# Products reordered by pass in a two-layer hybrid backbone, with a sub-layer's first product begun ahead of its last head tile

## The chip, the cores and the metric

One core of one Trainium2 chip runs the whole program in one launch. The metric is the device time of that launch in microseconds. Lower is better.

## The reference, cut to what matters

Two consecutive layers of a diffusion backbone act on 256 latent tokens and 256 context tokens of width 1024, in float32. Each layer is a feed-forward half-step, a token mixer, and a second feed-forward half-step, each modulated before and normalised after:

```
h = LN(x) * (1 + scale) + shift
a, u = split(h @ w_in)              # w_in: 1024 x 5632
y = (silu(a) * u) @ w_out           # w_out: 2816 x 1024
x = LN(alpha * x + 0.5 * gate * y) * g + b
```

Layer 0 mixes with a Fourier transform over half of the channels and a long convolution over the rest. Layer 1 mixes with two bidirectional gated scans (GLA with 4 heads of 64, HGRN2 with 4 heads of 128), and only its latent tokens go on to the last feed-forward half-step. The decay gate of GLA is a product of rank 16 per direction (`af @ a_up`).

## The kernel before, in words

The 512 tokens are four tiles of 128: tiles 0 and 1 are latents, 2 and 3 the context. `hT[k]` holds the modulated input of a sub-layer, feature-major, for eight blocks k of 128 features; each block is kept as a high part and a low part, both in the one-pass format `fp32r`. A weight unit (128 x 1024, 512 KB) is loaded by SP into one of three `raw` buffers; ScalarE (ACT) casts its high part (L78), and VectorE (DVE) subtracts to get the low part (L79). A float32 product is then three products that accumulate (`mm3`, L459): high x high, high x low, low x high. `Stream` (L39) keeps the order of the units: `get` takes the next one and splits up to two ahead, `split_to` and `split_spare` split further ahead. Units marked spare are split into the large pool `S`, the others into three buffers.

Everything is issued from one program order per engine, and each engine works its own list off in order. Background generators wait in `bg`; `step(n)` issues their next pieces between products, `flush()` issues all that is left.

A sub-layer starts with a head (`tm_head`, L522). It takes token tiles in turn: for tile t it runs four weight units against `hT` of that tile (24 products of 512 columns). In the meantime the last tiles are still being closed by `close` (L438): post-norm, norm (`xn`), transposes on TensorE (PE) into `ptr` (L411), scale and shift into `hm` (L428 on DVE or L430 on ACT), the split into `hT` (L226 on ACT, L227 on DVE or POOL). `due(t)` issues the transposes and what follows of tile t. In tile 2, `due(3)` is issued after the second unit (key `d`, L544) or, if the norm has not been issued by then, with a `flush()` at the key `F` (L548), and right behind it `split_to` splits the first units that follow the head (L551). After the head come the feature-major units (`fm_unit`, L464), each 24 products of 512 columns over all four tiles.

`tok_out` (L476) is the output projection: for each weight unit k all tiles of a pair, and for the last `tail` units tile by tile. `tm_mm` (L514) serves `tm_group` (L1364), the `rc` loop (L1443) and `chunk` (L1494).

The odd mixer (L1094) runs four `fm_lat` units (256 columns) for the queries, issues `due(2)` after the first (key `od2`, L1135), two more units with `due(3)` in each, and then the decay unit `pab` (L1152), which needs all four tiles of `hT`. `attend(j, tt)` (L1319) makes the scores `pF` on PE (L1331), masks them on DVE (`am`, L1338 to L1342), and forms `po` (L1348, L1351); for j = 0 the heads have 64 rows, two heads to a block of 128.

`mixer_close` (L1576) ends a mixer with `tok_out`, all of whose units are tail. In layer 1 it is followed by `ffn_lat`, whose head has eight units and two tiles.

Of the kernel before, what the change touches and what calls it, by code (L numbers as in the profile page):

```python
# [18 lines left out]
P = 128  # L19
# [109 lines left out]
def kernel(ctx: ExitStack, tc: tile.TileContext, a, out, stop=None):  # L129
# [346 lines left out]
    def tok_out(lhs, nk, tiles, fill=None, tail=0, done=None, cuts=None, hmajor=False):  # L476


        cols = {t: [slice(0, 512), slice(512, 1024)] for t in tiles}
        if cuts:  # L480
            cols[tiles[-1]] = cuts
        y = {t: [PS("y")[:, 0:c.stop - c.start] for c in cols[t]] for t in tiles}

        def mm(t, w, k, i):
            hh, hl = lhs(k, t)
            c = cols[t][i]
            mm3(y[t][i], hh, hl, w[0][:, c], w[1][:, c], k == 0, k == nk - 1)

        for k in range(nk - tail):
            w = ws.get()  # L490
            for t in tiles:
                for i in range(len(cols[t])):
                    mm(t, w, k, i)
            if fill:
                fill(k)
        held = {}
        last = ws.pos + tail
        limit = last
        while limit < len(ws.units) and ws.units[limit][2]:
            limit += 1  # L500
        ks = range(nk - tail, nk)
        for n, t in enumerate(tiles if tail else ()):
            nc_ = range(len(cols[t]))
            for i, (h, k) in enumerate([(h, k) for h in nc_ for k in ks] if n or hmajor else [(h, k) for k in ks for h in nc_]):
                if k not in held:
                    held[k] = ws.get(limit)
                mm(t, held[k], k, h)
                if fill and i % 2 and i < 2 * len(ks):
                    fill(ks[i // 2])
            if done:  # L510
                done(t, y[t])
        return y

    def tm_mm(y, w, kp, t):  # L514

        for kk in range(2):
# [3 lines left out]
            mm3(y, x[:, 0], x[:, 1], w[0][:, c], w[1][:, c], k == 0, k == KD - 1)  # L520

    def tm_head(tiles, done, n=1):  # L522

# [5 lines left out]
        for t in tiles:  # L529
# [57 lines left out]
    def ffn(l, i, extra=(), head=None):  # L587
# [7 lines left out]

        todo = (head or tm_head)(range(NT), done)
        bg.extend(extra)
        for f in range(2, KF):
# [3 lines left out]
            if f == 5 and stop == "head":  # L602
                return hs
            pa, pu = PS("pa"), PS("pu")
            fm_unit(pa)
            if todo:
# [253 lines left out]
    def even_mixer():  # L860
# [10 lines left out]

        tm_head(range(NT), done_a)

        def conv(g):

            for i in range(4):
                if i % 2 == 0:
                    pair = S([P, 2, T], name="cv")
                pu = PS("pu")
                fm_unit(pu)  # L880
                pv = pu.rearrange("p (s t) -> p s t", s=2)
# [203 lines left out]
    def queue_odd():  # L1085
        for f in range(17):
            ws.add(a["od_fm"][f], True, f < g_("SPN", 4), g_(f"qoi{f}", int(f in (1, 3, 4) or f > 5 and f % 2 == 1)))
        for n in range(4):
# [5 lines left out]
    def odd_mixer():  # L1094
        ab_c = Q([P, 2, 2], name="abc")
        sy.dma_start(out=ab_c, in_=a["gla_a_b"])
        aup = H([32, 2, 256], name="aup")
        sy.dma_start(out=aup, in_=a["gla_up"])
# [22 lines left out]
        def fm_lat(n):  # L1121

            o = PS("ql")[:, 0:L]
            hi, lo = ws.get()
            for k in range(KD):
                x = hT[k][:, :, 0:L]
                mm3(o, hi[:, P * k:P * k + P], lo[:, P * k:P * k + P], x[:, 0], x[:, 1], k == 0, k == KD - 1)
            step(n)
# [23 lines left out]
        pab = PS("pab")  # L1152
        fm_unit(pab)
        ab = H([32, T], name="ab")
        act.copy(ab, pab[0:32, :])
        E, U = [], []
# [162 lines left out]
        def attend(j, tt):  # L1319
# [5 lines left out]
            pa = [[PS("pF") for _ in range(nh // 2)] for _ in range(2)]  # L1325
            for n, f, r, hd in lst:
                for d in range(2):
                    qk, xx = QK[d, j], XX[d, j]
                    for c in (d, 1 - d):
                        kk = (qk if c == d else xx)[r, 1, f, P * tt:P * tt + P]  # L1330
                        pe.matmul(pa[d][n // 2][:, P * (n % 2) + 64 * c:P * (n % 2) + 64 * c + 64], lhsT=kk,  # L1331
                                  rhs=qk[r, 0, f, P * tt + 64 * c:P * tt + 64 * c + 64], start=True, stop=True)
            yield
            z = az[turn[0] % 2]
# [10 lines left out]
            po = [PS("po") for _ in range(nh // 2)]  # L1345
            for n, f, r, hd in lst:
                oc = po[n // 2][:, P * (n % 2):P * (n % 2) + P]
                pe.matmul(oc, lhsT=am[:, P * n:P * n + P], rhs=v[tt][:, P * hd:P * hd + P], start=True, stop=False)  # L1348
                for d in range(2):
                    s = 0 if (d == 0) == (tt == 0) else 1  # L1350
                    pe.matmul(oc, lhsT=XX[d, j][r, 0, f, P * tt:P * tt + P], rhs=ST[d, j][r, s, f, :],  # L1351
                              start=False, stop=d == 1)
            if j == 0:
# [222 lines left out]
    def mixer_close(l, tiles, nxt):  # L1576
# [7 lines left out]

        def done(t, y):
            if t == tiles[-1]:
                ws.split_spare(ws.pos + g_(f"{k0}a", 3))
                flush()
            else:
                ws.split_spare(ws.pos + g_(f"{k0}A{t}", 0))  # L1590
                older.append(t - 1)
            if t == tiles[0]:
# [10 lines left out]
        older = []  # L1603
        tok_out(lhs, KD, tiles, fill, KD, done, None, g_(f"{k0}h", 0))
# [209 lines left out]
def lay_out(inputs):  # L1814
# [66 lines left out]
    up[0:16, 0], up[16:32, 1] = i["gla_a_up"][0]  # L1881
    o["gla_up"] = up
    o["gla_a_b"] = i["gla_a_b"][0].reshape(2, 2, P).transpose(2, 0, 1)
# [28 lines left out]
```

## Time and profile before

| | us |
|---|---|
| median of 3 runs (1817.42 to 1825.67) | 1823.25 |
| the profiled execution's own time | 1824.63 |
| its span, first to last instruction | 1822.8 |

| engine | busy us | share | instructions |
|---|---|---|---|
| PE products | 1744.2 | 96% | 8204 |
| PE weight loads (overlap the products) | 1414.9 | 78% | 8204 |
| DVE | 1256.4 | 69% | 1818 |
| ACT | 713.3 | 39% | 1048 |
| POOL | 252.9 | 14% | 273 |

Each product is one record on PE, with a weight load of its own. A float32 product that is not in the one-pass format stands as two records. A record's duration includes its way through the array, so that successive records overlap: what a product costs in a stream is the time from its start to the next one's start. The chain that ended last names only the closing instructions of the program, so the stages are read from waits, windows and timelines.

### The profile page before, as it was taken

To read this page: it belongs to the slowest core of one execution; us is meant where nothing else is said; L and a number is where in the kernel's file an instruction comes from. 1 tells how busy PE (TensorE), PEld (TensorE's weight loads), DVE (VectorE), ACT (ScalarE), POOL (GpSimd) and SP (SyncE) were. 2 spreads that over 40 slices of the span, in tenths; PEclk is the share of its full clock that TensorE was granted. 3 is DMA by queue.
4 is the path that set the end of the run, shared out by engine and by line. 5 is a ranking of instruction groups with operands and counts; after the bars stand their busy time and mean duration, and the time that the engine had idled before them with its cause. 6 is when DMAs were issued, how large, how long until landed. Compare 5 with 4: busy or idle time off the path is not lost. (4 is left out here: it accounts for less than half of the span.)

```text
span 1822.8 us, 21896 instructions
## 1 busy us (share of the span) xinstructions
PE 1744.2 (96%) x8204; PEld 1414.9 (78%) x8204; DVE 1256.4 (69%) x1818; ACT 713.3 (39%) x1048; POOL 252.9 (14%) x273
## 2 busy tenths in 40 slices
PE   6999999998999999999999999999998999989998
PEld 5788888777766788888887788888877778767887
DVE  6788887676788677777477677733576594666755
ACT  5432233453323433323335423233355463444443
POOL 1223311011000111111001111111011241110000
PEclk9999999999999999999999999999999999889999
DMA  9645756653124055554655455435554223446664
GB/s 329 226 179 199 253 218 235 219 178 139 59 88 144 24 205 211 185 189 169 219 187 173 163 212 201 173 105 196 194 177 141 81 93 92 143 139 219 208 213 134
DMA packets 91498, 314.90 MB, mean 173 GB/s; under 512 B 10848, under 2 KB 11584, under 8 KB 91392
## 3 DMA queue, kind: packets, MB, share of 16 engines
q1 hardware_dynamic: 85952, 297.09, 47.0%
q0 software_dynamic: 4576, 15.91, 2.8%
q8 instruction: 64, 1.05, 0.2%
q10 hardware_dynamic: 864, 0.51, 0.1%
q14 instruction: 42, 0.34, 0.1%
HBM read 308.18 MB, written 4.24 MB: 171 GB/s over the span
## 5 line engine op out<-in xcount | busy, mean ns | idle before, releaser
L79 DVE TENSOR_TENSOR wlo<-raw,whi 128x1024 fp32r<-128x1024 f32 x332 | 415.3, 1254 | 321.6 <-ACT whi L78 321.4
L78 ACT CAST whi<-raw 128x1024 fp32r<-128x1024 f32 x332 | 346.8, 1051 | 338.5 <-PE y L462 122.8
L243 DVE SCALAR_TENSOR_TENSOR mt<-mraw,cb 128x1024 bf16<-128x1024 f32 x256 | 309.7, 1250 | 2.5 <-DMA mraw<-in_mod_w_dram 2.5
L462 PE MATMUL pu<-hT,wlo 128*128 128x512 f32 x576 | 224.7, 390 | 3.2 <-DVE wlo L79 3.2
L460 PE MATMUL pu<-hT,whi 128*128 128x512 f32 x576 | 225.7, 392 | 0.0
L461 PE MATMUL pu<-hT,whi 128*128 128x512 f32 x576 | 224.4, 390 | 0.0
L460 PE MATMUL pa<-hT,whi 128*128 128x512 f32 x480 | 187.8, 391 | 0.0
L462 PE MATMUL pa<-hT,wlo 128*128 128x512 f32 x480 | 187.1, 390 | 0.0
L461 PE MATMUL pa<-hT,whi 128*128 128x512 f32 x480 | 187.0, 390 | 0.0
L461 PE MATMUL y<-wlo,hh 128*128 128x512 f32 x468 | 183.2, 391 | 3.8 <-DVE wlo L79 3.8
L460 PE MATMUL y<-whi,hh 128*128 128x512 f32 x468 | 183.1, 391 | 0.0
L462 PE MATMUL y<-whi,hh 128*128 128x512 f32 x468 | 182.5, 390 | 0.0
L226 ACT CAST hh<-sa 128x256 fp32r<-128x256 f32 x120 | 42.8, 404 | 296.0 <-DVE sa L614 296.0
L227 POOL TENSOR_TENSOR hh<-sa,hh 128x256 fp32r<-128x256 f32 x120 | 86.3, 739 | 516.5 <-ACT hh L226 507.1
L462 PEld LDWEIGHTS pu<-hT,wlo 128*128 128x128 f32 x576 | 108.1, 188 | 26.6 <-DVE wlo L79 4.1
L460 PEld LDWEIGHTS pu<-hT,whi 128*128 128x128 f32 x576 | 108.1, 188 | 23.5 <-ACT hh L226 0.8
L461 PEld LDWEIGHTS pu<-hT,whi 128*128 128x128 f32 x576 | 108.2, 188 | 22.8 <-issue 0.5
L461 PEld LDWEIGHTS y<-wlo,hh 128*128 128x128 f32 x468 | 87.9, 188 | 24.9 <-DVE wlo L79 7.0
L460 PEld LDWEIGHTS pa<-hT,whi 128*128 128x128 f32 x480 | 90.1, 188 | 19.7 <-issue 0.9
L234 POOL TENSOR_TENSOR rstd<-rp,mhalf 128x1 f32<-128x1 f32 x42 | 35.4, 846 | 500.8 <-DVE rp L233 494.7
L462 PEld LDWEIGHTS pa<-hT,wlo 128*128 128x128 f32 x480 | 90.1, 188 | 18.8
L461 PEld LDWEIGHTS pa<-hT,whi 128*128 128x128 f32 x480 | 90.1, 188 | 18.5
(396 smaller groups left out, 3022.3 us busy)
## 6 DMA issues: line engine op xcount, KB each, us to landing
raw<-in_ffn_out_dram SPq DMA_DIRECT2D x154, 512.0 KB, 3.6
mraw<-in_mod_w_dram SPq DMA_DIRECT2D x144, 512.0 KB, 5.1
raw<-in_ffn_in_dram SPq DMA_DIRECT2D x120, 512.0 KB, 3.8
raw<-in_ffn_tm_dram SPq DMA_DIRECT2D x44, 512.0 KB, 4.2
raw<-in_od_fm_dram SPq DMA_DIRECT2D x17, 512.0 KB, 3.9
raw<-in_od_tm_dram SPq DMA_DIRECT2D x16, 512.0 KB, 3.3
raw<-in_ffn_head_dram SPq DMA_DIRECT2D x12, 512.0 KB, 4.3
raw<-in_ev_in_dram SPq DMA_DIRECT2D x12, 512.0 KB, 3.4
```

The lines of the kernel that those rows point to most:

```text
L78: self.nc.scalar.copy(hi, w)
L79: self.nc.vector.tensor_tensor(lo, w, hi.bitcast(F32), op=ALU.subtract)
L226: act.copy(dst_hi, src)
L227: (lo_eng or dve).tensor_tensor(dst_lo, src, dst_hi.bitcast(F32), op=ALU.subtract)
L234: gp.tensor_tensor(dst, t, mhalf.to_broadcast([P, n]), op=ALU.pow)
L243: dve.scalar_tensor_tensor(H([P, D], BF16, "mt"), w, 1.0, cb[s], op0=ALU.mult, op1=ALU.mult, accum_out=acc[:, s, b:b + 1])
L460: pe.matmul(o, lhsT=wh, rhs=xh, start=start, stop=False)
L461: pe.matmul(o, lhsT=wh, rhs=xl, start=False, stop=False)
L462: pe.matmul(o, lhsT=wl, rhs=xh, start=False, stop=stop)
```

## The change

- `fm_unit`, `fm_lat`, `tm_mm`, the body and the first tail tile of `tok_out`, and `tm_head` no longer run the three products of `mm3` together. They run all products of one pass (say high x high) and then all of the next.
- `first_unit`: after tile 2 of a head, the first feature-major unit is run for the columns of tiles 0 to 2 (384), and after tile 3 for the last 128 columns. It is used in both full feed-forward heads that go through `tm_head` and in the even mixer, three places.
- In these three heads `due(3)` is issued only after tile 2's last unit.
- `due(2)` in the odd mixer moves from after the first to after the third query unit.
- The decay unit is not split; it runs from the raw float32 weights, 32 columns wide, in four column groups of the array, 16 products instead of 24. The weights behind it are repeated four times, so that the sum over the groups is formed there.
- `attend` alternates between the row halves of two heads; for j = 0 one pause is gone.
- In `mixer_close` of layer 1 the splits ahead are issued from `fill`, unit by unit.

```diff
-    def fm_unit(o, view=lambda x: x):
-        hi, lo = ws.get()
-        for k in range(KD):
-            mm3(o, hi[:, P * k:P * k + P], lo[:, P * k:P * k + P], view(hT[k][:, 0, :]), view(hT[k][:, 1, :]), k == 0, k == KD - 1)
+    def fm_unit(o, c=slice(0, T), w=None):
+        w = w or ws.get()
+        for n, (a_, b_) in enumerate(((0, 0), (0, 1), (1, 0))):
+            for k in range(KD):
+                pe.matmul(o[:, c], lhsT=w[a_][:, P * k:P * k + P], rhs=hT[k][:, b_, c], start=n + k == 0, stop=n == 2 and k == KD - 1)
+        return w
...
+        def block(todo):
+            for a_, b_ in ((0, 0), (1, 0), (0, 1)):
+                for t, w, k, i in todo:
+                    pe.matmul(y[t][i], lhsT=lhs(k, t)[a_], rhs=w[b_][:, cols[t][i]], start=k + a_ + b_ == 0, stop=k == nk - 1 and b_ == 1)
...
+    OLD, NEW = slice(0, 3 * P), slice(3 * P, T)
+    def first_unit(name):
+        part = []
+        def begin():
+            part.append(PS(name))
+            part.append(fm_unit(part[0], OLD))
+        def end():
+            fm_unit(part[0], NEW, part[1])
+            return part[0]
+        return begin, end
+    def tm_head(tiles, done, n=1, between=None):
...
-            for u in range(4 * n):
+            order = ((0, 0), (1, 0), (0, 1)) if t == tiles[0] else ((0, 0), (0, 1), (1, 0))
+            for v in range(12 * n):
+                p_, u = divmod(v, 4 * n)
                 if u not in w:
                     w[u] = ws.get(limit)
-                tm_mm(y[u // 4], w[u], u % 4, t)
+                for kk in range(2):
+                    k = 2 * (u % 4) + kk
+                    pe.matmul(y[u // 4], lhsT=hT[k][:, order[p_][0], P * t:P * t + P], rhs=w[u][order[p_][1]][:, 512 * kk:512 * kk + 512],
+                              start=p_ == 0 and k == 0, stop=p_ == 2 and k == KD - 1)
+                if v % 3 < 2:
+                    continue
+                u = v // 3
...
-                if u == g_(f"{k0}d{t}", 4 * n - 3):
+                if u == g_(f"{k0}d{t}", 4 * n - 3) and not (between and t == tiles[-2]):
                     due(t + 1)
...
-                if t == tiles[-2] and u == g_(f"{k0}F", 4 * n - 2):
+                if t == tiles[-2] and u == (4 * n - 1 if between else g_(f"{k0}F", 4 * n - 2)):
                     flush()
                     due(t + 1)
                     ws.split_to(ws.pos + g_(f"{k0}A", 1))
             if todo:
                 run(todo)
             todo = done(t, *y)
+            if between and t == tiles[-2]:
+                between()
...
-            if i == g_("od2", 0):
+            if i == g_("od2", 2):
                 due(2)
...
-        fm_unit(pab)
+        w = ws.get()
+        for n in range(2):
+            for k in range(KD):
+                j = k % 4
+                pe.matmul(pab[32 * j:32 * j + 32, :], lhsT=w[:, P * k:P * k + 32], rhs=hT[k][:, n, :].bitcast(F32),
+                          start=n == 0 and k < 4, stop=n == 1 and k >= 4, tile_position=(0, 32 * j))
...
-            yield
+            if j:
+                yield
...
+            if l and "y" not in seen:
+                ws.split_to(first + (4, 5, 7, 8, 9, 10, 11, 11)[k])
```

## Rows read from the trace of the kernel before

**Rows 1.** The page, part 1: busy us, share of the span, instructions.

```profile
PE 1744.2 (96%) x8204; PEld 1414.9 (78%) x8204; DVE 1256.4 (69%) x1818; ACT 713.3 (39%) x1048; POOL 252.9 (14%) x273
```

**Rows 2.** Waits of PE, whole run: us in total, times, longest.

```profile
PE ptr L411 <- ACT xn L398: 13.1, 10, 4.8
PE hd L460 <- ACT hT L226: 9.0, 6, 5.4
PE y L461 <- DVE lo L79: 4.8, 7, 1.1
...
PE pt L900 <- DVE cv L886: 4.4, 3, 2.2
...
PE y L461 <- DVE wlo L79: 4.2, 8, 0.8
PE pu L462 <- DVE wlo L79: 3.2, 2, 1.7
...
PE ya L461 <- DVE wlo L79: 1.7, 3, 0.8
```

**Rows 3.** Timeline of PE, from four stretches: start, us, then engine, line, tiles, count.

```profile
447.11 0.39 PE L460 MATMUL hd<-hi,hT 128*128 128x512 f32 x1
447.34 0.39 PE L461 MATMUL hd<-lo,hT 128*128 128x512 f32 x1
...
1390.07 0.28 PE L462 MATMUL ql<-hT,lo 128*128 128x256 f32 x1
1390.19 0.28 PE L460 MATMUL ql<-hT,hi 128*128 128x256 f32 x1
...
1511.04 0.39 PE L1331 MATMUL pF<-qk 128*128 128x64 f32 x2
1511.27 0.39 PE L1331 MATMUL pF<-qk,xx 128*128 128x64 f32 x2
...
21.96 1.52 PE L1661 MATMUL pm<-mraw,cst 128*32 128x128 f32 x48
```

**Rows 4.** Windows: length, then busy per engine, PEclk, DMA share, GB/s.

```profile
439.50:443.70 4.20, 4.14 (x15) 3.33 (x16) 1.37 (x4) 3.04 (x7) 0.30 (x1) 0.60 0.01 4
...
500.00:568.00 68.00, 60.41 (x226) 42.02 (x225) 60.42 (x76) 19.45 (x28) 2.18 (x4) 0.95 0.29 93
1376.00:1381.00 5.00, 0.16 (x3) 0.04 (x1) 4.27 (x9) 0.90 (x2) 0.55 (x1) 0.80 0.38 118
1381.00:1385.50 4.50, 4.50 (x21) 4.50 (x22) 3.00 (x5) 4.44 (x12) 0.00 (x0) 0.50 0.81 318
1563.00:1580.00 17.00, 17.00 (x68) 14.36 (x68) 8.57 (x15) 3.37 (x5) 2.63 (x4) 0.51 0.39 132
```

**Rows 5.** Timelines of PE and ACT at tile 3 of the three heads.

```profile
439.51 1.77 PE L411 MATMUL ptr<-ident,xn 128*128 128x128 f32 x8 [2.52 <-ACT xn L398]
...
443.73 2.96 ACT L78 CAST whi<-raw 128x1024 fp32r<-128x1024 f32 x3
...
641.04 1.04 PE L411 MATMUL ptr<-ident,xn 128*128 128x128 f32 x8
...
645.14 2.00 ACT L78 CAST whi<-raw 128x1024 fp32r<-128x1024 f32 x2
...
1016.75 1.37 PE L411 MATMUL ptr<-ident,xn 128*128 128x128 f32 x8 [0.44 <-ACT xn L398]
...
1020.57 2.01 ACT L78 CAST whi<-raw 128x1024 fp32r<-128x1024 f32 x2
```

**Rows 6.** Timelines of ACT and PE, odd mixer up to the decay unit.

```profile
1393.61 1.52 ACT L398 ACTIVATE xn<-x,nb,rstd 128x512 f32<-128x512 f32 x2 [1.04 <-DVE nb L388]
...
1406.54 0.39 PE L462 MATMUL pab<-hT,wlo 128*128 128x512 f32 x1
```

**Rows 7.** Timelines of PE and ACT, last attention and last head.

```profile
1562.83 0.46 PE L1348 MATMUL po<-vg,am 128*128 128x128 f32 x2 [2.10 <-DVE am L1342]
...
1610.82 2.92 ACT L78 CAST hi<-raw 128x1024 fp32r<-128x1024 f32 x3
```

More of the change, by code (lines that the diff above doesn't have):

```diff
@@ L503, in tok_out @@
             nc_ = range(len(cols[t]))
+            if not n and not hmajor:
+                for i, k in enumerate(ks):
+                    held[k] = ws.get(limit)
+                    block([(t, held[k], k, h) for h in nc_])
+                    if fill:
+                        fill(k)
+                if done:
+                    done(t, y[t])
+                continue
             for i, (h, k) in enumerate([(h, k) for h in nc_ for k in ks] if n or hmajor else [(h, k) for k in ks for h in nc_]):
@@ L519, in tm_mm @@
             x = hT[k][:, :, P * t:P * t + P]
-            mm3(y, x[:, 0], x[:, 1], w[0][:, c], w[1][:, c], k == 0, k == KD - 1)
-    def tm_head(tiles, done, n=1):
+            for n in range(2):
+                pe.matmul(y, lhsT=x[:, n], rhs=w[0][:, c], start=n + k == 0, stop=False)
+        for kk in range(2):
+            k = 2 * kp + kk
+            pe.matmul(y, lhsT=hT[k][:, 0, P * t:P * t + P], rhs=w[1][:, 512 * kk:512 * kk + 512], start=False, stop=k == KD - 1)
+    OLD, NEW = slice(0, 3 * P), slice(3 * P, T)
[9 more added lines that the diff above has]
+    def tm_head(tiles, done, n=1, between=None):
         w = {}
@@ L594, in done @@
             return to_features(slice(P * (t % 2), P * (t % 2) + P), [hs[t // 2][0]], h)
-        todo = (head or tm_head)(range(NT), done)
+        if head:
+            todo = head(range(NT), done)
+        else:
+            begin, end = first_unit("pa")
+            todo = tm_head(range(NT), done, 1, begin)
         bg.extend(extra)
@@ L603, in ffn @@
                 return hs
-            pa, pu = PS("pa"), PS("pu")
-            fm_unit(pa)
+            if f == 2 and not head:
+                pa = end()
+            else:
+                pa = PS("pa")
+                fm_unit(pa)
+            pu = PS("pu")
             if todo:
@@ L870, in done_a @@
             split(at[t][:, 0], at[t][:, 1], y)
-        tm_head(range(NT), done_a)
+        begin, end = first_unit("pu")
+        tm_head(range(NT), done_a, 1, begin)
         def conv(g):
@@ L878, in conv @@
                     pair = S([P, 2, T], name="cv")
-                pu = PS("pu")
-                fm_unit(pu)
+                if g + i == 0:
+                    pu = end()
+                else:
+                    pu = PS("pu")
+                    fm_unit(pu)
                 pv = pu.rearrange("p (s t) -> p s t", s=2)
@@ L1123, in fm_lat @@
             o = PS("ql")[:, 0:L]
[L1124 to L1127, printed above, removed]
+            w = ws.get()
+            for m, (a_, b_) in enumerate(((0, 0), (1, 0), (0, 1))):
+                for k in range(KD):
+                    pe.matmul(o, lhsT=w[a_][:, P * k:P * k + P], rhs=hT[k][:, b_, 0:L], start=m + k == 0, stop=m == 2 and k == KD - 1)
             step(n)
@@ L1152, in odd_mixer @@
         pab = PS("pab")
-        fm_unit(pab)
-        ab = H([32, T], name="ab")
-        act.copy(ab, pab[0:32, :])
+        w = ws.get()
+        for n in range(2):
+            for k in range(KD):
+                j = k % 4
+                pe.matmul(pab[32 * j:32 * j + 32, :], lhsT=w[:, P * k:P * k + 32], rhs=hT[k][:, n, :].bitcast(F32),
+                          start=n == 0 and k < 4, stop=n == 1 and k >= 4, tile_position=(0, 32 * j))
+        ab = H([P, T], name="ab")
+        act.copy(ab, pab)
         E, U = [], []
@@ L1325, in attend @@
             pa = [[PS("pF") for _ in range(nh // 2)] for _ in range(2)]
[L1326 to L1332, printed above, removed]
-            yield
+            for d, c, (n, f, r, hd) in [(d, c, p) for f in range(2) for d in range(2) for c in (d, 1 - d) for p in lst if p[1] == f]:
+                qk, xx = QK[d, j], XX[d, j]
+                kk = (qk if c == d else xx)[r, 1, f, P * tt:P * tt + P]
+                pe.matmul(pa[d][n // 2][:, P * (n % 2) + 64 * c:P * (n % 2) + 64 * c + 64], lhsT=kk,
+                          rhs=qk[r, 0, f, P * tt + 64 * c:P * tt + 64 * c + 64], start=True, stop=True)
+            if j:
+                yield
             z = az[turn[0] % 2]
@@ L1585, in done @@
         def done(t, y):
+            seen["y"] = t
             if t == tiles[-1]:
-                ws.split_spare(ws.pos + g_(f"{k0}a", 3))
+                if not l:
+                    ws.split_spare(ws.pos + g_(f"{k0}a", 3))
                 flush()
-            else:
+            elif not l:
                 ws.split_spare(ws.pos + g_(f"{k0}A{t}", 0))
+            if t != tiles[-1]:
                 older.append(t - 1)
@@ L1881, in lay_out @@
     up[0:16, 0], up[16:32, 1] = i["gla_a_up"][0]
-    o["gla_up"] = up
+    o["gla_up"] = np.tile(up, (4, 1, 1))
     o["gla_a_b"] = i["gla_a_b"][0].reshape(2, 2, P).transpose(2, 0, 1)
```

25 lines of the change are left out of this document (14 added, 11 removed).

## The prediction

> **What bounds the kernel now.** I read the page first: PE works on products for 96% of the span [rows 1], so there are 78.6 us in which it does not, and a change can win from these, from products that get cheaper, and from the granted clock. Then the waits of PE, which say whose lateness makes up those microseconds [rows 2]: norms of the tiles that are closed last (`ptr`), `hT` of the tile that a head takes next (`hd`), and low parts of weights (`lo`, `wlo`). Then windows, for what an idle PE loses besides [rows 4]: after the 2.5 us wait before 439.5 the granted clock is 0.60 for 4.2 us, after the wait of 1376 to 1381 it is 0.50 for 4.5 us. These are stretches at 1.2 GHz rather than 2.4; the first one lost 4.2 x (1 - 0.60) = 1.7 us of work. Last the timelines, for the order behind each wait.
>
> **What a product costs.** In a stream one starts every 0.23 us at 512 columns and every 0.12 at 256 (447.11 to 447.34, 1390.07 to 1390.19) [rows 3]. On a straight line that is 0.175 at 384 and 0.065 at 128. But products of only 64 columns start every 0.11 (two records in 0.23) [rows 3], so there is a floor which is not one of columns; for 128 I take 0.11, with 0.065 and 0.23 (no cheaper than 512) as ends. Reordering by pass leaves the number of products as it is, and each has its own weight load before and after: zero, within 0.01 us a product either way for the stationary operand that no longer repeats.
>
> The Trainium skill ("TensorE: Matmul & The Clock Gate", section "Back-to-back issue gap") gives 81 ns for a sustained stream at 128 columns; by that figure, an estimate, the sum would be 2 us lower. For 512 columns it gives 131 ns where the rows here have 230, so the rows decide.
>
> **Low parts needed later.** In the body of `tok_out` a unit's low part is now needed after 8 products, not 1, 1.6 us later; in `chunk` and in the first tail tile after 4. No single wait there is over 1.1 us. `y<-wlo` is 4.2 us in 8 waits [rows 2], of which I count five, 2.6 us, as body and gone; `ya<-wlo` 1.7, gone. `y<-lo` 4.8 us is in the tails, where each next unit arrives by DMA slower than PE asks; there the later need is earned once per tail, 3 x 0.23 = 0.7, and in two of three tails the head behind it waits for a norm whose DVE chain starts from those splits, so it is lost again: 0.7 in all. `pu<-wlo` 3.2 us is in the even mixer, where DVE is busy 60.4 of 68 us and the convolution's transposes wait for it anyway (`pt<-cv`, 4.4) [rows 2, 4]: zero. Sum: **-5.0** (0 to -9, with all of `y<-lo` and `pu`).
>
> **The three heads.** This is where I expect the loss. `flush`, `due(3)` and `split_to` stand in this order in the program before and after. So ACT casts the first unit's high part only behind tile 3's `hT`: at 443.73, 645.14 and 1020.57, done 1.0 us later, while the transposes end at 441.28, 642.08 and 1018.12 [rows 5]. Before, half of tile 2 or a quarter of it lay behind those transposes and filled that time; now all of tile 2 lies ahead, and what lies behind is the early product, which needs just that cast. PE idles 3.4 + 4.1 + 3.4 = 10.9 us, and tile 3's `hT` is ready before the early product starts, so the product covers nothing. Idle of that length has cost 1.7 us of clock [rows 4]: 3 x 1.7 = 5.1. The split itself: 24 x (0.175 + 0.11 - 0.23) = 1.4, three times 4.2 (0.3 to 12.6 by the ends above). What goes: the 2.5 us wait before 439.51 with its 1.7 of clock, 0.4 before 1016.75 [rows 5], and about 1.0 of what `hd<-hT` has besides its longest [rows 2]; 5.6. Sum 10.9 + 5.1 + 4.2 - 5.6 = **+14.6**. Queued behind the new wait is all of PE's list, tile 3's head first; ACT and DVE wait for PE only afterwards. No DMA moves in SP's or POOL's queue: the units' loads are issued by buffers that come free.
>
> **Odd mixer.** `due(2)` two units later: these are 2 x 24 x 0.12 = 5.8 us of PE work in front of a norm that is 4.8 us late [rows 2], so that wait and its 2.2 us of clock go [rows 4]. ACT's and DVE's pieces of tile 2 then stand behind tile 3's, whose norm comes some 2 us sooner than 1393.61 [rows 6]; but PE is at tile 3's transposes by about 1389, since the last query unit before them is ready then. A new wait of 3.5 us with 1.1 of clock takes its place. The decay unit: 24 x 0.23 = 5.5 before; after, `pm` has the same form at 128 columns, 48 records, 24 products, in 1.52 us, six rounds of four at 0.25 [rows 3], so four rounds at 512 columns are 4 x 4 x 0.25 = 4.0. Its raw buffer stays taken until it has run, under a window with DMA to spare. Sum -4.8 - 2.2 - 1.5 + 4.6 = **-3.9** (-9 to 0), to be read at the unit's end, 1406.54 before [rows 6].
>
> **Attention and last head.** For j = 0 each `pF` group is 32 records at 0.11; two row halves in turn can at best halve it, 1.8 us, twice; `po` about as much. These 17 us run at 0.51 [rows 4], so up to 10 us. One pause less also means one stretch of `rc` products less between `pF` and `po`, so the 2.10 wait for `am` [rows 7] grows by about a microsecond. In the last head PE waits 5.4 us for `hT` of tile 0 [rows 2] while three casts of 2.92 us stand before it on ACT [rows 7]; with the splits issued from `fill` they are done earlier, about 3 us. But the pass order wants all eight units' high parts within 16 products, 3.7 us, and only four are split by then; the casts of the other four are 4 x 1.0, and their low parts stand on DVE before the closing of tile 1, so tile 1's norm is late instead, and only 3 products, not 6, lie behind its transposes. I take **-4.5** (-11 to 0).
>
> **Sum.** -5.0 + 14.6 - 3.9 - 4.5 = +1.2 against the profiled execution's 1824.6; the median of the runs stands 1.4 below that execution, so 1823.25 + 1.2 = 1824.5. A half per cent, 9.1 us, is about what a measurement of this kernel can tell from no change. The clocks of three heads are the term with the freest choice; with half of it the sum is 1822, without it 1819. I forecast **1823**, no change.
>
> **Rivals.** *The head's cover works*: the cast of the first unit lands before the transposes end, or PE arrives so late that it is done. Then idle and clock, 16.0 us, go and only the split is paid: 1823 - 16 = 1807, faster. Against it is the order on ACT in all three heads [rows 5]; for it, only that PE may come later than before. Nearly the same time results if the odd mixer and the last head reach their outer ends (-9 and -11, 1811). *Slower: the clock stays low.* In 1563 to 1580 PE was busy for all 17 us and still had 0.51 [rows 4]. If after the head's new idle the clock stays at 1.2 GHz through the early product and tile 3, 4.2 + 5.5 us, that costs 9.7 instead of 1.7 per head: 1823 + 24 = 1847. It decides from 3 us per head. Against it: 439.5 to 443.7 recovered within 512-column products. *The column groups don't run at once*: each product then takes a whole round's 4 x 0.25 = 1.0, so 16 us instead of 4.0, 1835; the `pm` row speaks against it. The Trainium skill ("FP8 and Floating Point Precision", section "TensorE Precision Notes") states four passes through the array for a true float32 product; by that rule and without groups the unit would be a loss.
>
> **How the numbers follow.** Forecast 0.44. Cover works or outer gains: 0.33, faster. Clock 0.13, column groups 0.03, and a 128-column product at 0.23 with small gains elsewhere (+8.4, and the odd mixer at 0 gives 1835) 0.07: slower 0.23. The range reaches to both sides of the forecast's until a tenth is left out at each end: 1800 (cover and outer gains together come to 1795) to 1837. The likeliest case's own range is 1814 to 1832.
>
> **What would show it.** Heads: PE idle of 3 to 4 us between tile 3's transposes and the first 384-column product, released by ACT's cast at L78, clock near half behind it; 128-column products every 0.11. If that idle is absent the forecast's largest term is wrong. Odd mixer: no wait at tile 2's transposes, one at tile 3's, `pab` about 4 us long. `y<-wlo` and `ya<-wlo` near zero; `pu<-wlo` gone, with `pt<-cv` grown. Last head: wait for `hT` near 2.5 us and a longer one before tile 1's transposes.

## The result and the profile after

| | before | after |
|---|---|---|
| median of the runs, us | 1822.73 (4 runs, 1817.42 to 1825.67) | 1835.69 (4 runs, 1833.43 to 1837.62) |
| the profiled execution's own time, us | 1824.63 | 1833.43 |
| its span, us | 1822.8 | 1831.6 |

The changed kernel is slower: the ratio of its runs to those of before is 1.0065, with a 95% interval of 1.0048 to 1.0082. The medians are 13.0 us apart, the two profiled executions 8.8.

The page of the changed kernel, part 1, answers to [rows 1]:

```profile
PE 1747.5 (95%) x8284; PEld 1421.4 (78%) x8284; DVE 1253.0 (68%) x1817; ACT 715.2 (39%) x1047; POOL 253.2 (14%) x273
```

PE is busy only 3.3 us longer, in a span that is 8.8 us longer. The rest is waiting. The waits of PE over the whole run (columns as in [rows 2]):

```profile
PE ptr L411 <- ACT xn L398: 10.2, 5, 3.9
PE po L1411 <- DVE am L1404: 8.2, 2, 4.9
PE pa L469 <- ACT whi L78: 7.8, 2, 4.2
PE pt L958 <- DVE cv L944: 7.2, 3, 3.4
PE hd L580 <- ACT hi L78: 5.0, 4, 2.6
PE hd L580 <- ACT hT L226: 4.0, 3, 2.1
...
PE pu L469 <- ACT whi L78: 3.6, 1, 3.6
...
PE y L495 <- DVE lo L79: 0.6, 2, 0.4
```

The waits of `y`, `ya` and `pu` for low parts that [rows 2] list (4.8, 4.2, 3.2 and 1.7 us) are down to 0.6 for `lo` and 0.4 or less for `wlo`. In their place stand `pa` and `pu` waiting for a high part (11.4 us in three waits), `po` waiting for `am` (8.2 instead of 2.1) and longer waits for `cv` (7.2 instead of 4.4); `y` waits 3.2 us for high parts, where it waited 0.3.

**Where it was lost.** To see the place, the same instruction of ACT, DVE or POOL was paired in the two profiled executions and its start after minus its start before taken, with the median over 20 us. This is how far behind the changed kernel is at the end of each stretch:

| stretch (times of before) | behind at its end, us | lost (+) or won (-) |
|---|---|---|
| start to 60 us | 1.7 | +1.7 |
| body of the first `tok_out`, to 360 | -0.1 | -1.8 |
| first tail and first head, to 500 | 2.5 | +2.6 |
| convolution, to 540 | 4.3 | +1.8 |
| rest of the even mixer, to 620 | 3.8 | -0.5 |
| second head, to 680 | 9.8 | +6.0 |
| body of the second `tok_out`, to 960 | 7.7 | -2.1 |
| second tail, to 1000 | 8.8 | +1.1 |
| third head, to 1060 | 12.7 | +3.9 |
| body of the third `tok_out`, to 1340 | 11.2 | -1.5 |
| third tail, odd mixer, to 1500 | 6.8 | -4.4 |
| scans and attention, to `tok_out`'s first product | 6.1 | -0.7 |
| last mixer's end and eight-unit head, to the first `ya` | 10.6 | +4.5 |
| to the end | 8.8 | -1.8 |

Two of the ends are products of PE: `tok_out` starts at 1585.8 before and 1591.9 after, `ya` at 1646.2 and 1656.8. The last row ends with the span.

**The heads.** PE and ACT at tile 3 of the first head, the timelines that answer to [rows 5]:

```profile
439.20 1.36 PE L411 MATMUL ptr<-ident,xn 128*128 128x128 f32 x8 [0.24 <-ACT xn L398]
444.12 4.60 PE L469 MATMUL pu<-hT,whi 128*128 128x384 f32 x16 [3.56 <-ACT whi L78]
...
455.43 1.90 PE L469 MATMUL pu<-hT,whi 128*128 128x128 f32 x16
...
441.98 1.14 ACT L226 CAST hT<-hm 128x512 fp32r<-128x512 f32 x2
443.01 2.96 ACT L78 CAST whi<-raw 128x1024 fp32r<-128x1024 f32 x3
```

The 2.5 us wait ahead of the transposes is down to 0.24, and a wait of 3.56 stands behind them. ACT works off tile 3's `hT` and only then casts the high part that the early product needs. When that product starts, tile 3's `hT` is ready, so it covers nothing. In the other two heads the wait is 4.2 and 3.56. The windows behind the three waits (columns as in [rows 4]):

```profile
444.10:448.50 4.40, 4.38 (x16) 4.38 (x17) 4.40 (x4) 2.35 (x3) 1.09 (x1) 0.62 0.26 86
...
651.90:656.00 4.10, 4.10 (x15) 4.10 (x16) 3.79 (x4) 2.11 (x3) 0.00 (x0) 0.58 0.41 141
...
1030.90:1034.50 3.60, 3.60 (x12) 3.60 (x13) 3.60 (x5) 2.11 (x3) 0.90 (x2) 0.54 0.63 203
```

These are stretches of full work at a clock of 0.62, 0.58 and 0.54, which makes 4.40 x 0.38 + 4.10 x 0.42 + 3.60 x 0.46 = 5.1 us more.

**Odd mixer.** PE at tile 3, answering to [rows 6]:

```profile
1404.00 1.97 PE L411 MATMUL ptr<-ident,xn 128*128 128x128 f32 x8 [3.91 <-ACT xn L398]
...
1410.63 3.64 PE L1215 MATMUL pab<-hT,raw 128*32 128x512 f32 x32
1414.20 0.97 PE L469 MATMUL pf<-hT,whi 128*128 128x512 f32 x3
```

The wait has moved from tile 2 (4.84) to tile 3 (3.91). From the first query product to the decay unit's end it takes 30.0 us (1384.2 to 1414.2) instead of 33.7 (1373.1 to 1406.8), and 2.5 of the 3.7 are the decay unit itself (6.1 to 3.6).

**Attention.** PE and DVE in the two tiles of j = 0, answering to [rows 7]:

```profile
1567.77 1.20 PE L1411 MATMUL po<-vg,am 128*128 128x128 f32 x4 [3.27 <-DVE am L1404]
...
1577.61 0.61 PE L539 MATMUL rc<-lo,hT 128*128 128x512 f32 x2
1583.10 1.19 PE L1411 MATMUL po<-vg,am 128*128 128x128 f32 x4 [4.88 <-DVE am L1404]
...
1574.09 3.50 DVE L79 TENSOR_TENSOR lo<-raw,hi 128x1024 fp32r<-128x1024 f32 x3 [5.86 <-ACT hi L78]
1579.66 1.23 DVE L79 TENSOR_TENSOR wlo<-raw,whi 128x1024 fp32r<-128x1024 f32 x1 [2.08 <-ACT whi L78]
1580.80 1.43 DVE L1400 COPY_PREDICATED az<-masks,pF 128x256 f32<-128x256 int32 x4
1582.27 0.69 DVE L1404 TENSOR_TENSOR am<-az 128x512 f32<-128x512 f32 x1
...
1578.58 1.04 ACT L78 CAST whi<-raw 128x1024 fp32r<-128x1024 f32 x1 [2.64 <-DMA raw<-in_od_out_dram]
```

The scores are almost twice as quick: a group of 32 records spans 1.73 us where it took 3.12. The Trainium skill ("TensorE: Matmul & The Clock Gate", section "Part 3: Packing small matmuls - row/col tiling") says that products in different row groups of the array run at once; the trace agrees, with a factor of 1.8. But with one pause less, six `rc` products are all that PE has between the scores and `po`, and the second tile's masks stand on DVE behind a low part, which waits for a cast whose raw weights arrive by DMA 2.64 us after ACT is free. PE waits 4.88 us there, where it did not wait at all before, and behind either wait the clock is 0.50:

```profile
1567.80:1573.00 5.20, 5.20 (x26) 4.21 (x27) 0.43 (x1) 0.54 (x3) 0.00 (x0) 0.50 0.08 32
...
1583.10:1587.70 4.60, 4.60 (x25) 3.70 (x25) 1.76 (x6) 0.00 (x0) 2.63 (x4) 0.50 0.45 159
```

From the first scores of j = 0 to `tok_out` it takes 31.0 us, before 31.4.

**Last head.** DVE and PE at the end of the last mixer:

```profile
1602.50 1.23 DVE L79 TENSOR_TENSOR lo<-raw,hi 128x1024 fp32r<-128x1024 f32 x1 [2.10 <-ACT hi L78]
1604.87 1.23 DVE L79 TENSOR_TENSOR lo<-raw,hi 128x1024 fp32r<-128x1024 f32 x1 [1.14 <-ACT hi L78]
1606.01 0.69 DVE L227 TENSOR_TENSOR hT<-pt,hT 128x512 fp32r<-128x512 f32 x1
1606.61 1.22 DVE L79 TENSOR_TENSOR lo<-raw,hi 128x1024 fp32r<-128x1024 f32 x1
1607.74 0.69 DVE L331 TENSOR_TENSOR z<-y,gate 128x512 f32<-128x512 f32 x1
...
1601.42 1.05 ACT L78 CAST hi<-raw 128x1024 fp32r<-128x1024 f32 x1 [5.24 <-DMA raw<-in_ffn_tm_dram]
...
1618.67 1.97 PE L411 MATMUL ptr<-ident,xn 128*128 128x128 f32 x8 [3.91 <-ACT xn L398]
1622.74 6.13 PE L580 MATMUL hd<-hi,hT 128*128 128x512 f32 x14 [2.10 <-ACT hT L226]
1630.74 5.98 PE L580 MATMUL hd<-hi,hT 128*128 128x512 f32 x18 [1.87 <-ACT hi L78]
```

Tile 0's last product ends at 1603.6, but its post-norm (`z`, L331) starts 4.2 us later, at 1607.74, because the low parts that `fill` asks for come first on DVE, and their casts had waited for the raw weights. Before, `z` followed 1.6 us behind the product. The waits of PE there, in the kernel before:

```profile
1610.26 1.74 PE L411 MATMUL ptr<-ident,xn 128*128 128x128 f32 x8 [1.62 <-ACT xn L398]
1617.41 0.80 PE L460 MATMUL hd<-hi,hT 128*128 128x512 f32 x1 [5.41 <-ACT hT L226]
```

So the wait for tile 0's `hT` is shorter, 2.10 instead of 5.41 us, but the one for its norm is longer, 3.91 instead of 1.62, and two are new: 1.87 us for a high part (1630.74 above) and 1.74 for tile 1's norm (at 1640.72, before 0.15). From `tok_out`'s first product to `ya` it takes 65.0 us instead of 60.5.

### The profile page after: what moved, and what is told of

Read it like the earlier page. It is cut to its first block, busy times and chain, and to the rows that moved or that the text cites. A ratio compares the mean times of both kernels' runs of the same rounds, so it can differ in the third digit from the quotient of the medians.

```text
span 1831.6 us, 22092 instructions
## 1 busy us (share of the span) xinstructions
PE 1747.5 (95%) x8284; PEld 1421.4 (78%) x8284; DVE 1253.0 (68%) x1817; ACT 715.2 (39%) x1047; POOL 253.2 (14%) x273
## 5 line engine op out<-in xcount | busy, mean ns | idle before, releaser
L469 PE MATMUL pu<-hT,whi 128*128 128x512 f32 (+2 forms) x1168 | 277.1, 390 | 3.6 <-ACT whi L78 3.6
L469 PE MATMUL pa<-hT,whi 128*128 128x512 f32 (+2 forms) x992 | 233.7, 389 | 7.8 <-ACT whi L78 7.8
L495 PE MATMUL y<-whi,hh 128*128 128x512 f32 x924 | 229.8, 390 | 1.7 <-ACT whi L78 1.6
L495 PEld LDWEIGHTS y<-whi,hh 128*128 128x128 f32 x924 | 172.6, 188 | 39.2 <-ACT whi L78 3.8
L469 PE MATMUL pu<-hT,wlo 128*128 128x512 f32 (+2 forms) x584 | 143.0, 387 | 0.4 <-DVE wlo L79 0.4
L495 PE MATMUL y<-wlo,hh 128*128 128x512 f32 x462 | 124.1, 390 | 0.2
L469 PE MATMUL pa<-hT,wlo 128*128 128x512 f32 (+2 forms) x496 | 119.8, 384 | 0.0
L79 DVE TENSOR_TENSOR lo<-raw,hi 128x1024 fp32r<-128x1024 f32 x63 | 80.5, 1290 | 39.2 <-ACT hi L78 38.8
L78 ACT CAST hi<-raw 128x1024 fp32r<-128x1024 f32 x63 | 65.2, 1056 | 37.9 <-DMA raw<-in_ffn_out_dram 16.9
L580 PE MATMUL hd<-hi,hT 128*128 128x512 f32 x256 | 70.5, 424 | 9.0 <-ACT hi L78 5.0
```

What stands on the lines that cost most here:

```text
L78: self.nc.scalar.copy(hi, w)
L79: self.nc.vector.tensor_tensor(lo, w, hi.bitcast(F32), op=ALU.subtract)
L469: pe.matmul(o[:, c], lhsT=w[a_][:, P * k:P * k + P], rhs=hT[k][:, b_, c], start=n + k == 0, stop=n == 2 and k == KD - 1)
L495: pe.matmul(y[t][i], lhsT=lhs(k, t)[a_], rhs=w[b_][:, cols[t][i]], start=k + a_ + b_ == 0, stop=k == nk - 1 and b_ == 1)
L580: pe.matmul(y[u // 4], lhsT=hT[k][:, order[p_][0], P * t:P * t + P], rhs=w[u][order[p_][1]][:, 512 * kk:512 * kk + 512], start=p_ == 0 and ...
```

## The experiments

**Is it the heads?** In the changed kernel the three heads go as before (no early product); the order by pass stays.

```diff
-            todo = tm_head(range(NT), done, 1, begin)
+            todo = tm_head(range(NT), done)
...
         def end():
-            fm_unit(part[0], NEW, part[1])
+            part.append(PS(name))
+            fm_unit(part[0])
```

> The changed kernel with its three heads as before (no early product, due(3) and the flush where they were, first feature-major unit whole), the order by pass kept. Theory A (the loss is made where the early product waits for the first unit's cast): the three idles of 3.7, 4.3 and 3.7 us ahead of the 384-column products go, with the stretches near half clock behind them; some of the old waits for tile 3's norm come back; about 12 us less than the changed kernel, 1823 (1819 to 1828). Rival B (the heads lose by the order by pass itself, which wants all four units' high parts first): the loss stays, 1832 or more, with waits for the high parts in its place.

Measured: 1822.94 us (10 runs), ratio to before 1.0002 (0.9987 to 1.0018). Theory A's number. The three waits for a first unit's high part are gone, the wait for tile 3's norm is back in the first head (2.82 us at 439.5), and in the table's manner the heads lose 0.3, -0.9 and -0.9 instead of 2.6, 6.0 and 3.9: the early product as issued costs 14.0 us in the profiles. The waits for high parts that rival B names exist (4.9 us), but cost little net.

**Can the cover work?** One split is issued between the norm and tile 3's transposes.

```diff
                     flush()
+                    if between:
+                        ws.split_to(ws.pos)
                     due(t + 1)
                     ws.split_to(ws.pos + g_(f"{k0}A", 1))
```

> The changed kernel with the first unit's split issued between the flush and due(3), so that its cast stands on ScalarE ahead of tile 3's scaling and hT. Theory A: the cast runs while TensorE transposes, each of the three idles falls below 0.6 us and the early product then covers tile 3's chain; the idles (11.8) and their clock (about 5) go, the split's own price (about 1.6 per head) stays: 1819 (1815 to 1824). Rival C (the wait only moves: the low part stands on VectorE ahead of tile 3's scaling, so tile 3's head waits for hT behind the early product): 1829 or more, with waits for hT of 2 to 4 us per head at tile 3.

Measured: 1820.31 us (10 runs), ratio 0.9996 (0.9980 to 1.0012): 15 us less than the changed kernel by the medians. PE and ACT in the first head:

```profile
439.52 1.36 PE L411 MATMUL ptr<-ident,xn 128*128 128x128 f32 x8
441.16 3.07 PE L469 MATMUL pu<-hT,whi 128*128 128x384 f32 x16 [0.28 <-ACT whi L78]
...
445.45 2.01 PE L580 MATMUL hd<-hi,hT 128*128 128x512 f32 x8
...
440.08 1.03 ACT L78 CAST whi<-raw 128x1024 fp32r<-128x1024 f32 x1
441.01 1.49 ACT L430 ACTIVATE hm<-ptr,modc 128x128 f32<-128x128 f32 x4
443.67 1.14 ACT L226 CAST hT<-hm 128x512 fp32r<-128x512 f32 x2 [1.17 <-DVE hm L428]
```

The cast runs beside the transposes, the product starts 0.28 us behind them, and tile 3's head follows it without a wait: `hT`, 1.7 us later than it was, is still early enough. The other heads wait 0.54 and not at all. Rival C falls, and theory A's number nearly comes: 1820.31 where it said 1819. The early product in two parts takes 441.16 to 445.45, 4.29 us, and 2.63 for the last 128 columns, 6.9 us instead of the 5.4 of a whole unit (24 x 0.227).

**Attention: the pause.** The pause between scores and masks is back, the alternation stays.

```diff
-            if j:
-                yield
+            yield
             z = az[turn[0] % 2]
```

> The changed kernel with the pause between scores and masks for j = 0 back, the alternating row halves kept. Theory A (the scores got cheaper, but the masks now stand behind less TensorE work, so po waits for them): the two waits for am, 3.3 and 4.9 us, fall to 3 us in sum or less; about 4 us less, 1832. Rival D (VectorE is late with the masks wherever they are issued, because of the low parts ahead of them): the waits keep 7 us or more in sum and the time stays within 1 us, 1835.

Measured: 1826.44 us (4 runs), ratio 1.0042 (1.0027 to 1.0057). The waits for `am` fall from 8.2 to 3.9 us in sum (theory A said 3 or less), so rival D falls. The stretch goes from 31.0 to 20.3 us, more than twice what theory A asked for, because the clock does not fall. The windows of scores and `po` in both tiles:

```profile
1566.00:1574.00 8.00, 5.77 (x48) 4.41 (x46) 7.97 (x21) 4.48 (x5) 2.05 (x2) 1.00 0.50 182
1574.20:1576.70 2.50, 2.44 (x24) 2.11 (x26) 2.50 (x3) 1.05 (x1) 0.00 (x0) 1.00 0.20 31
1576.70:1581.50 4.80, 4.80 (x48) 3.94 (x44) 2.79 (x5) 2.23 (x4) 0.00 (x0) 1.00 0.85 307
1582.90:1587.00 4.10, 4.03 (x36) 3.38 (x36) 2.03 (x7) 1.39 (x5) 2.63 (x4) 1.00 0.38 120
```

By the medians the gain is 9.3 us, by the ratios (whose intervals overlap) 4. The masks still stand behind that low part on DVE here; what the pause changes is how much work PE has between the scores and `po`.

**Last head: the splits.** The splits at the mixers' ends are issued as before.

```diff
-                if not l:
-                    ws.split_spare(ws.pos + g_(f"{k0}a", 3))
+                ws.split_spare(ws.pos + g_(f"{k0}a", 3))
...
-            if l and "y" not in seen:
-                ws.split_to(first + (4, 5, 7, 8, 9, 10, 11, 11)[k])
```

> The changed kernel with the splits at the end of the mixers issued as before (behind the tiles, not from fill). Theory A (the low parts issued from fill stand on VectorE ahead of tile 0's post-norm, which starts 4.3 us behind its product instead of 1.7): the stretch from the first product of tok_out to the first of ya falls from 65.0 us to about 61; 1832. Rival E (the eight-unit head loses by the order by pass, which wants eight high parts early): the stretch stays at 64 to 66, 1835.

Measured: 1833.83 us (4 runs), ratio 1.0086 (1.0068 to 1.0103). The time doesn't tell it from the changed kernel. The stretch does: 62.3 us instead of 65.0, with tile 0's wait for the norm back at 1.40 us and the wait for its `hT` back at 5.79. Theory A holds for 2.7 of the 4.5 us; the other 1.8 are looked for below.

**The alternation alone, in the kernel before.** Only the order of the products in `attend` is taken over.

```diff
-            for n, f, r, hd in lst:
-                for d in range(2):
...
+            for d, c, (n, f, r, hd) in [(d, c, p) for f in range(2) for d in range(2) for c in (d, 1 - d) for p in lst if p[1] == f]:
```

> The kernel before with one thing of the change: attend's alternation of the row halves, its pause kept. Theory A (two half-height products in turn run in the time of one, and with half the work behind it the stretch of po keeps the full clock): the stretch from the first scores to tok_out's first product falls from 31.4 us to 20 to 23, with a granted clock near 1.0 instead of 0.51; about 9 us less than before, 1814. Rival F (the clock falls behind the wait for am as it did before, and stays down through the second tile): the products halve but run at half clock, the stretch keeps 27 us or more, 1819 or more.

Measured: 1817.6 us (10 runs), ratio 0.9984 (0.9970 to 0.9998). The stretch takes 24.2 us, with a granted clock of 0.79: between the two theories. The wait for `am` is 3.4 us and the clock falls behind it for some microseconds, not for both tiles.

**The order by pass alone, in the kernel before.** `fm_unit`, `fm_lat`, `tm_mm`, `tok_out` and `tm_head` as in the change, all else as before.

```diff
-            mm3(o, hi[:, P * k:P * k + P], lo[:, P * k:P * k + P], view(hT[k][:, 0, :]), view(hT[k][:, 1, :]), k == 0, k == KD - 1)
...
+        for n, (a_, b_) in enumerate(((0, 0), (0, 1), (1, 0))):
+            for k in range(KD):
```

> The kernel before with the order by pass alone (feature-major units, query units, tok_out's body and first tail tile, heads, rc and chunk): no early product, due(2), decay unit, attend and the splits of the last mixer as before. Theory A (it removes waits for low parts in the bodies, about 5.5 us, and gives some back in the first head, the convolution and the eight-unit head): 1820 (1816 to 1823). Rival G (the waits only move, from low parts to high parts and norms): 1822 to 1827.

Measured: 1815.48 us (10 runs), ratio 0.9972 (0.9958 to 0.9987). Better than theory A, and rival G falls. In its profile the three bodies win 2.4, 2.1 and 1.5 us, about as in the changed kernel; what theory A had not counted is the attention, 23.8 us instead of 31.4: the wait for `am` is 0.5 us there, and the granted clock over the stretch 0.93. So 7.6 of the 11.3 us between the two profiles come from a stretch in which the order by pass touches only the `rc` products.

**All three mends.** Cover, pause and old splits together.

> The changed kernel with three mends: the first unit's split between flush and due(3), the pause in attend back, and the last mixer's splits issued as before. Theory A (the three losses are separate and add up): 15 for the heads, 10 for the attention and 2 to 3 for the last head less than the changed kernel's 1836, 1808 (1803 to 1813), faster than both kernels. Rival H (they share one slack, so that what one gives the next wait takes): 1815 or more.

Measured: 1807.49 us (6 runs), ratio 0.9935 (0.9915 to 0.9955). The losses are separate and add up: 15.4, 9.3 and 1.9 by the medians make 26.6, and 28.2 were measured. Rival H falls, and the kernel is faster than both.

**The eight-unit head unit by unit.**

```diff
-                p_, u = divmod(v, 4 * n)
+                p_, u = (v % 3, v // 3) if n > 1 else divmod(v, 4 * n)
```

> As the kernel with three mends, and the eight-unit head of the last layer goes unit by unit again instead of pass by pass. Theory A (by pass that head wants eight high parts within 16 products): the stretch from tok_out's first product to the first of ya falls from about 62.3 us to 60.5 or less, 1806. Rival I (the stretch is set by the norms of the two tiles, whatever the order of the products): within 0.5 us of the other.

Measured: 1807.18 us (6 runs), ratio 0.9928 (0.9911 to 0.9945). The stretch falls from 62.9 us to 60.3, as theory A has it; the time is the same within its interval. So the order by pass costs this head 2.6 us, which with the 2.7 of the splits accounts for its loss of 4.5 and a little more.

**The convolution's units by block.** The three passes go block by block again in seven of the convolution's units.

```diff
+        if by_k:
+            for k in range(KD):
+                mm3(o, w[0][:, P * k:P * k + P], w[1][:, P * k:P * k + P], hT[k][:, 0, :], hT[k][:, 1, :], k == 0, k == KD - 1)
+            return w
...
-                    fm_unit(pu)
+                    fm_unit(pu, by_k=True)
```

> As the kernel with three mends and the eight-unit head unit by unit, and the convolution's feature-major units run by block again (high, high with low, low with high of one block after another) instead of by pass. Theory A (by pass the short waits for low parts become one wait of 3.7 us at the convolution's transposes, behind which the inverse transform's products lose 1.9 us of clock): the first wait at the transposes falls to about 0.7 us, two waits of 1.7 to 1.9 us for low parts come back, the products of po<-yf,raw start every 0.43 us again instead of 0.67; 1.5 us less than without it, 1805.5. Rival J (VectorE sets the stage, so nothing changes): the stage's end stays where it is within 0.5 us.

Measured: 1804.7 us (6 runs), ratio 0.9898 (0.9878 to 0.9919), the lowest median here, though its interval overlaps with that of the kernel that it edits. Paired with that kernel in the table's manner, the convolution ends 2.6 us earlier. PE at the convolution's transposes, first in the changed kernel:

```profile
521.41 1.34 PE L958 MATMUL pt<-ident,cv 128*128 128x128 f32 x9 [3.42 <-DVE cv L944]
522.57 5.29 PE L1023 MATMUL po<-yf,raw 128*128 128x512 f32 x8
```

and with the units by block:

```profile
516.51 1.31 PE L964 MATMUL pt<-ident,cv 128*128 128x128 f32 x9 [0.55 <-DVE cv L950]
517.66 3.60 PE L1029 MATMUL po<-yf,raw 128*128 128x512 f32 x8
```

The sum of the waits is the same: 1.69 and 1.57 us for low parts and 0.55 here, 3.81 in all, against 0.40 for a low part and 3.42 here, 3.82 in all. But the one long wait is followed by products at a lower clock: 5.29 us for eight that otherwise take 3.60 (5.42 in the kernel that is edited, behind the same 3.42). Rival J falls.

**Is a covered early product worth having?** The same kernel as the one with the eight-unit head mended, without the early product.

> As the kernel with three mends and the eight-unit head unit by unit, but without the early product: heads issued as before, the first feature-major unit whole. Theory A (once its cast is in time, the early product buys back tile 3's waits, 2.5 us and its clock in the first head and about 2 us in the third, and pays 1.6 us per head for 384 and 128 columns in place of 512): 1 to 2 us slower than with the covered early product, 1808.5. Rival K (covered, it is worth the whole wait for tile 3 in each head): 4 us or more slower, 1811 or more.

Measured: 1810.72 us (6 runs), ratio 0.9931 (0.9914 to 0.9949). The ratios don't tell it from the kernel with the covered product; the medians say 3.5 us. In the profiles the first head loses 2.4 us, the second wins 1.6 and the third loses 0.6: 1.4 us in all, theory A's size, and too little for rival K. Most of the difference lies elsewhere: the attention, which this edit does not touch, takes 24.3 us instead of 20.4, with a wait for `am` of 3.40 us instead of 2.49 and a lower clock behind it. So what the covered product is worth is known from the profiles of the heads alone.

**The odd mixer's two steps undone.**

```diff
-            if i == g_("od2", 2):
+            if i == g_("od2", 0):
...
-        w = ws.get()
-        for n in range(2):
...
+        fm_unit(pab)
```

> The changed kernel with the odd mixer as before in two things: due(2) after the first query unit, the decay unit split and run in 24 products of 512 columns over the whole array. Theory A (the change gained there about what was forecast): the stretch from the first query product to the decay unit's end goes from 30.0 us back to about 34, a wait of about 4.8 us at tile 2's transposes takes the place of the one of 4.1 at tile 3's, the decay unit takes 5.5 to 6.1 us instead of 3.6. Rival L (the two waits are worth the same and the decay unit's gain is lost in the next wait): the stretch stays at 30 to 31.

Measured: 1841.43 us (1 run). PE there:

```profile
1397.23 1.97 PE L411 MATMUL ptr<-ident,xn 128*128 128x128 f32 x8 [5.90 <-ACT xn L398]
...
1417.00 3.93 PE L469 MATMUL pab<-hT,whi 128*128 128x512 f32 x16 [1.14 <-ACT hT L226]
1420.76 1.98 PE L469 MATMUL pab<-hT,wlo 128*128 128x512 f32 x8
1422.58 1.75 PE L469 MATMUL pf<-hT,whi 128*128 128x512 f32 x7
```

The stretch is 34.3 us, the wait at tile 2 is 5.90, the decay unit takes 5.6. Theory A holds, rival L falls.

**Both kernels profiled again.** No edit; the question is how steady the attention's clock is.

> The kernel before, unedited, profiled a second time. What is asked: whether its attention runs at half clock in every execution. Theory M (it does in some executions only): the stretch from the first scores of j = 0 to tok_out's first product is about 24 us instead of 31.4 when its granted clock is near 1.0, and the execution's time is then below 1820. Rival N (it always does): 31 us at 0.5, whatever the time.

> The kernel before, unedited, profiled a third time; the same two theories: M, a stretch of about 24 us wherever the granted clock there is near 1.0, with a time below 1820; N, 31 us at 0.5 in every execution.

> The changed kernel, unedited, profiled a second time. Theory M for it: its two waits for am, 3.3 and 4.9 us, bring the half clock in every execution, so the stretch stays at 31 us; the three idles of the heads are 3.5 us or more again. Rival N: stretch and idles differ by more than 2 us from the first profile.

Measured: in two more executions of the kernel before (1829.95 and 1824.33 us) the stretch takes 29.8 and 28.3 us, against 31.4. The wait for `am` is 2.10 us each time; what differs is how long the half clock lasts behind it: 17, 14 and 10 us in the three profiles. So neither theory holds whole: the half clock is in each of the three, and the stretch varies by 3 us with it. The changed kernel's second profile (1834.3 us) repeats the first: 30.9 us, waits that agree within 0.3 us, and the same idles in the heads (3.56, 4.19 and 3.56).

## Why the prediction was wrong

The forecast was no change (1823), from a sum of +1.2 us; the measured time lies near the upper end of the range, and the case that came, slower, had 0.23. Step by step:

- **Low parts needed later, forecast -5.0.** The three bodies and the last stretch won 1.8 + 2.1 + 1.5 + 1.8 = 7.2 us. The tails lost about 0.7 net and the convolution 1.8: -4.7. That the sum came out is luck: the bodies won more than was counted, 5.4 us where 2.6 stood (what the rest of it comes from is not shown), and the tails and the convolution, set at a gain of 0.7 and at zero, lost that much again. "Zero" for `pu<-wlo` was wrong: the wait did move to the transposes, as said, and there it was one long wait instead of three short ones, with a clock loss behind it.
- **The three heads, forecast +14.6.** Right in mechanism and size: waits 3.6 + 4.2 + 3.6 = 11.4 (forecast 10.9), clock 5.1 (5.1), the split 1.5 per head (1.4), 128 columns at 0.108 to 0.112 (0.11 taken). The Trainium skill's 81 ns for 128 columns ("TensorE: Matmul & The Clock Gate", section "Back-to-back issue gap") was not reached. The stretches lost 12.5 in all, and undoing the early product gives 14.0 back. Two readings on the way were not right. The 0.11 us for 128 columns came out by luck: it was taken from `pF`, where 0.11 is the distance of two records, and a float32 product there is two records, so one of 64 columns costs 0.23. And the low end of the split's price, 0.3, is that of one head; three make 0.7.
- **Odd mixer, forecast -3.9.** Measured -3.7: the new wait at tile 3 is 3.91 (3.5 said), the decay unit 3.6 us long (4.0). It took 6.1 before, not 5.5.
- **Attention and last head, forecast -4.5 (-11 to 0).** This step failed: -0.4 and +4.5, so +4.1, which is 8.6 us off and outside its own range. Two parts of it. The wait for `am` was to grow "by about a microsecond"; the first did (2.10 to 3.27), but the second tile, which had not waited before, waits 4.88, since nothing was asked about what stands ahead of its masks on DVE. Behind both waits the clock falls, which eats what the quicker scores give. And the splits issued from `fill` were to be "done earlier, about 3 us". The wait for tile 0's `hT` did fall by 3.3 us, to 2.10 (near 2.5 was said). But the casts were earlier only in the program: their raw weights had not come, so ACT and DVE, working in order, held tile 0's norm behind them, and its wait grew by 2.3 us. The order by pass cost 2.6 us more there: tile 1's late norm had been foreseen, but had no number in the sum.

With what was measured the four steps make -4.7 + 12.5 - 3.7 + 4.1 = +8.2 us. The two profiled executions are 8.8 apart; the rest is +1.7 at the start and -1.1 in stretches that the four steps do not name. The start needs no cause in the change: the two further profiles of the kernel before are 4.6 and 0.9 us behind the first one by 60 us. The medians are 13.0 apart, since the profiled execution of before lies 1.9 us above its median and that of the changed kernel 2.3 below.

Of the rivals, "the head's cover works" describes what one moved line makes of the change, not the change. "The clock stays low" did not happen in the heads: it was back within 4.4 us. "The column groups don't run at once" asked for 16 us in the decay unit, which takes 3.6. The slower result came from none of them, but from the forecast case with its last term reversed. That term lumped two gains whose conditions, DVE's list ahead of the masks and the arrival of raw weights, stood in the trace of before and were not read for the second tile.

What stays open: how much the pause is worth in the time. The ratios say 4 us, the medians 9.3. In the profiles the stretch is 29.5 to 31.3 us in the six executions without the pause (the changed kernel twice, without the early product, with the cover, with the old splits, with the odd mixer's steps undone), 20.3 to 20.4 in four with alternation and pause, and 24.2 and 24.3 in two more (the alternation alone, and the last of the kernels without the early product), where the first wait for `am` is 3.40 us instead of 2.49. No run moves the low part that stands ahead of the masks on DVE, so that part of the account is read from the timelines alone.

## What to carry to other kernels

Work that is meant to cover another engine's chain must have its own inputs queued ahead of that chain on every engine it shares: here one split moved by one line took away a loss of 14 us, and what the covered product then wins over none is 1.4 us in the profiles, too little for the times to show. Issuing something earlier in the program is a delay for all that stands behind it, if its data comes by DMA and is not there yet. And count a wait of PE with what it does to the clock behind it: several short waits can be cheaper than one long wait of the same sum.

## What was not expected of the hardware

- After a wait of 2.10 us in the attention the granted clock stayed at 0.51 for 17 us of unbroken work in the kernel before, a stretch of half-height products and short float32 ones; with the row halves alternating and a longer wait, 2.49 us, at the same place it was 1.00 throughout in the kernel with the pause. The same program differs from one execution to the next in how long the half clock lasts there (17, 14 and 10 us, in stretches of 31.4, 29.8 and 28.3 us).
- The executions of the kernel before differ with the clock: the mean granted clock was 0.992 in the one of 1815.35 us and 0.983 in the one of 1827.65. So a few microseconds of difference in clock behind one wait, which the profile of one execution shows, can be absent in the next.
- Four 32-column groups ran at once in float32 at 512 columns: 32 records, which are 16 products, in 3.57 us (1410.63 to 1414.20). That is 0.89 us for a round of four products, where one product of 512 columns in the one-pass format takes 0.227.
